# Where a pair's KT transposes stand among its scores, and a pause between two products of the joins

## The chip, the core and the metric

The kernel runs on one core of a Trainium2 chip. The metric is the device time of one execution in microseconds. A separate profiled execution gives the page of the profile and the trace. PE is TensorE, DVE is VectorE, ACT is ScalarE, POOL is GpSimd and SP is SyncE.

## The reference

One layer of a hybrid trunk over 16 + 512 = 528 tokens of width 1024. A combined projection feeds an RWKV-7 branch (eight heads of 64), a forgetting-attention branch (eight heads of 64) and the gates. Their gated sum and a residual follow, then an MLP with squared ReLU.

```python
u = rmsnorm(h, norm_mix[l])
proj = u @ w_in[l]
...
y_rw = rwkv7_branch(feat_rw, ...)
y_fx = fox_branch(feat_fx, b_f[l], q_gain[l], k_gain[l])
merged = gates[..., :D_MODEL] * (y_rw @ w_out_rw[l]) + gates[..., D_MODEL:] * (y_fx @ w_out_fx[l])
h = h + (merged @ w_o[l]).astype(h.dtype)
z = rmsnorm(h, norm_mlp[l])
h = h + (jnp.square(jax.nn.relu(z @ w_up[l])) @ w_down[l]).astype(h.dtype)
```

The part that the change touches is the recurrence of the RWKV-7 branch:

```python
def step(S, inp):
    rt, wt, kt, vt, at, bt = inp
    sa = jnp.einsum('bhij,bhj->bhi', S, at)
    S = S * wt[:, :, None, :] + sa[..., None] * bt[:, :, None, :] + vt[..., None] * kt[:, :, None, :]
    yt = jnp.einsum('bhij,bhj->bhi', S, rt)
    return S, yt
```

## The kernel before

The first stage computes everything from the input norm to the two branches and the gates; the later stages are the output projections and the MLP. The change lies in the first stage.

**The recurrence in chunks.** Tokens are padded to nine chunks of 64. The eight heads form four pairs, and two pairs form a group, so that there are two groups. For each pair, `keys` (L900) makes the scaled keys: BK on DVE (L922) and POOL, and on DVE (L924) KT, which is BK times the chunk's last decay. `rows` (L928) makes the left sides L0 and L1. `scores` (L952) then does, for three chunks at a time, 12 products of BK with L into two banks named psr (L964). DVE reads them out, masked, into Bm (L965) and back into L (L967, two operations). It also transposes KT of the same three chunks into a bank pbt (L971), from which ACT copies bkT in three operations (L972 and L974). bkT is read only by the chain.

`inverse` (L976) inverts, for a whole group, the triangular blocks which Bm holds. DVE first inverts blocks of 16 (L1001 and L1002), in tiles that take over the places of BK and KT; POOL clears the one at KT's place (L984 and L985). The joins then put the blocks together with products on PE of 32 rows: a first product p1 from Bm and Dn (L1027), read by DVE into W2 (L1028); a second, p1 from Tt and W2 (L1033); a third, p2 from W2 and Tt (L1036). DVE adds the second to Dn (L1037) and the third to Tt (L1041). Two more products follow (L1049 and L1056). `chain` (L1060) then goes through the nine chunks one after the other.

**Who sets the order on PE.** Within this stage the order of PE's instructions is the program's order, which a planner in the kernel writes while the program is built. Each piece of work is a generator. Between two yields it issues one *visit*, a few products and what reads them. The yielded function tells when, by the planner's clock, the next visit could start: when its inputs are ready and its PSUM banks are free. `Turns.run` (L167) takes the first stream, by rank, whose time plus a room for its rank isn't past the clock, and then books the issued instructions (`ck.read`, L186):

```python
ROOM = {0: 0.0, 1: 0.8, 2: 1.5, 3: 1.5, 4: 2.5, 8: 0.5}
...
at = next((i for i, t in enumerate(times) if t + self.ROOM[self.streams[i][0]] <= ck.pe + ck.SLACK), None)
```

SLACK is 0.15. The ranks are 0 for a chain, 1 for the recurrence's preparation (`recurrent`, L1187, with all of `keys`, `rows`, `scores` and `inverse`), 2 for attention, 3 for attention's features, 4 for the group norms and the splitting of results, and 8 for the input projections (L556). A visit of the projections is three or six products of the lines L582, and needs only its weights and a bank of its own.

The planner books DVE, ACT, POOL and the DMA with a fixed and a per-column time (L68); a product on PE by its columns and the size of its tile (L127), with 0.1 where the tile's shape changes. Operations that write a `wlo`, the rest of a weight after its upper half is taken off, are booked on POOL (L116); they are issued to DVE. The order on DVE, ACT and POOL is not the planner's but that of the framework's own scheduling.

**PSUM.** The tag "sm" has four banks, shared by psr, pbt, pw and most others. `banks(n)` (L507) gives the time at which the n oldest of the ring are free. The projections use "pj" (two banks) and borrow two more while no chain runs.

**The queues.** The projections' weights come over SP's DMA queue. Neither `scores` nor `inverse` issues a DMA.

Of the kernel before, what the change touches and what calls it, by code (L numbers as in the profile page):

```python
# [24 lines left out]
NCH = 9  # L25
# [30 lines left out]
def bc(ap, dim, n):  # L56

    shape = list(ap.shape)
    shape.insert(dim, n)
    return ap.unsqueeze(dim).to_broadcast(shape)  # L60
# [129 lines left out]
def kernel(ctx, tc, ht, x, win, par, cst, gain, lora, wout, wo, wup, wdn, out, dbg=None):  # L190
# [97 lines left out]
    with ExitStack() as st:  # L288
# [5 lines left out]
        def psm(name="psm"):  # L294
            return ps.tile([128, 512], F32, name=name, tag="sm", bufs=4)
# [22 lines left out]
        ck = Clock(nc)  # L318
# [188 lines left out]
        def banks(n):  # L507
            return ck.ring("sm", n, 4)
# [346 lines left out]
        class Pair:  # L855
# [96 lines left out]
            def scores(self):  # L952


                BK, L, KT = self.BK, self.L, self.KT
                self.bkT = bkT = kp.tile([128, NCH, 128], F32, name="bkT", bufs=2)
                self.Bm = Bm = kp.tile([128, NCH, 128], F32, name="Bm", bufs=2)
                for c0 in range(0, NCH, 3):
                    yield lambda: max(ck.ready(BK, *L) if c0 == 0 else 0.0, banks(2))
                    sb, sk = [psm("psr").rearrange("p (a b) -> p a b", b=128) for e in range(2)]  # L960
                    for j in range(3):
                        for sp, row, turn in ((sb, 0, 1), (sk, 1, -1)):
                            for (e, hs), os in zip(enumerate(hss), hss[::turn]):
                                mm(sp[os, j, :], BK[hs, c0 + j, row, :], L[e][hs, c0 + j, :], start=True, stop=True)  # L964
                    V.tensor_tensor(Bm[:, c0:c0 + 3, :], sb[:, :3, :], bc(tmask, 1, 3), ALU.mult)  # L965
                    for e, os in enumerate(hss[::-1]):
                        V.tensor_tensor(L[e][os, c0:c0 + 3, :], sk[os, :3, :], bc(tmask[os], 1, 3), ALU.mult)  # L967
                    yield lambda: max(ck.ready(KT) + 1.0, banks(1))
                    pb = psm("pbt").rearrange("p (a b) -> p a b", b=128)
                    for c in range(c0, c0 + 3):  # L970
                        nc.tensor.transpose(pb[:, c - c0, :], KT[:, c, :, :].rearrange("p a b -> p (a b)"), ident)  # L971
                    A.copy(bkT[:, c0:c0 + 3, :64], pb[:, :3, :64])  # L972
                    for hs, os in zip(hss, hss[::-1]):
                        A.copy(bkT[hs, c0:c0 + 3, 64:], pb[os, :3, 64:])  # L974

        def inverse(g, Bms, late):  # L976
# [40 lines left out]
            def half(q):  # L1017
                return qs[q % 2]
# [12 lines left out]
            for n, pr_, c in cells:  # L1031
                for e, hs in enumerate(hss):
                    mm(p1[hs, n, :], Tt[qs[2 * e], c, pr_, :], W2[qs[2 * e], n, :], start=True, stop=True)  # L1033
            for n, pr_, c in cells:
                for q in range(4):
                    mm(p2[qs[q], n, :], W2[qs[q], n, :], Tt[qs[q], c, pr_, half(q)], start=True, stop=True)  # L1036
# [150 lines left out]
        def recurrent():  # L1187
# [4 lines left out]
            for g in range(2):  # L1192
                prs = pairs[2 * g:2 * g + 2]
                for j, q in enumerate(prs):
# [19 lines left out]
                    if j == 0 and g > 0:  # L1214
                        yield normalised[0][1]
                    yield from q.bonus()
                yield from inverse(g, [q.Bm for q in prs], (lambda: pairs[2].ask_keys(inverted[0])) if g == 0 else lambda: None)
                inverted[g].done = True
                turns.add(0, chain(g, prs))
# [396 lines left out]
```

## Time and profile before

| what | value |
|---|---|
| median of three runs | 828.11 us (827.68 to 828.64) |
| profiled execution | 826.71 us |
| its span, first to last instruction | 824.9 us |
| mean granted clock of TensorE | 0.998 |
| first stage, 0 to 400 us: PE, DVE, ACT busy | 388.30, 298.40, 250.04 us |
| 400 to 495 us: PE, DVE, ACT busy | 93.92, 55.61, 48.35 us |
| 495 us to the end: PE, DVE, ACT busy | 325.94, 253.75, 154.10 us |

The visits of the scores (L964) lie at 52.6 to 60 us for pair 0, 84.8 to 94 for pair 1, 209.9 to 224 for pair 2 and 251.3 to 259 for pair 3. The joins' products (L1027 to L1056) lie at 114 to 130 us and at 283 to 299 us.

In a line of the time line the first number is the start in microseconds, the second the duration; a group of like instructions is merged, with its count behind an x. In brackets stand the idle time of the engine before it, and who ended it. The products are pipelined, so that what one costs is read from the start of one to the start of the next, not from its duration. A product of fp32 operands appears as more than one PE instruction.

### The profile page before, as it was taken

To read this page: it belongs to the slowest core of one execution; us is meant where nothing else is said; L and a number is where in the kernel's file an instruction comes from. 1 tells how busy PE (TensorE), PEld (TensorE's weight loads), DVE (VectorE), ACT (ScalarE), POOL (GpSimd) and SP (SyncE) were. 2 spreads that over 40 slices of the span, in tenths; PEclk is the share of its full clock that TensorE was granted. 3 is DMA by queue.
4 is the path that set the end of the run, shared out by engine and by line. 5 is a ranking of instruction groups with operands and counts; after the bars stand their busy time and mean duration, and the time that the engine had idled before them with its cause. 6 is when DMAs were issued, how large, how long until landed. Compare 5 with 4: busy or idle time off the path is not lost.

```text
span 824.9 us, 15506 instructions
## 1 busy us (share of the span) xinstructions
PE 808.1 (98%) x5886; PEld 667.3 (81%) x5886; DVE 607.8 (74%) x1196; ACT 452.5 (55%) x941; POOL 120.0 (15%) x124
## 2 busy tenths in 40 slices
PE   8999999998999999999999999999999999999998
PEld 6979887876987886778788889888888888888886
DVE  6797985687779855975267655875698678867988
ACT  7767548766575457664366534664445434543452
POOL 1021000010011000000022003100740174017400
PEclk9999999999999999999999999999999999999999
DMA  7222221211211311223687404533742365236532
GB/s 240 75 71 79 69 92 56 79 40 65 79 52 54 128 46 61 90 66 116 218 289 226 159 0 151 176 82 100 225 150 87 115 221 150 77 118 208 156 107 76
DMA packets 51483, 95.88 MB, mean 116 GB/s; under 512 B 5832, under 2 KB 7240, under 8 KB 51408
## 3 DMA queue, kind: packets, MB, share of 16 engines
q1 hardware_dynamic: 47680, 86.37, 33.0%
q0 software_dynamic: 1280, 4.20, 1.7%
q10 hardware_dynamic: 2448, 4.33, 1.5%
q8 instruction: 46, 0.75, 0.4%
q14 instruction: 29, 0.24, 0.1%
HBM read 88.56 MB, written 6.31 MB: 115 GB/s over the span
## 4 chain that ended last, share of the span: by engine, by line
PE 86%; DVE 5%; ACT 5%; issue 2%; DMA 1%; POOL 0%; DVEq 0%; ACTq 0%; SPq 0%
PE pj L582 22%; PE po L1357 21%; PE po L1484 12%; PE pd L1484 5%; PE po L1267 4%; PE po L1329 3%; PE pj L394 1%; PE pd L1298 1%; PE po L1298 1%; PE psc L751 1%; PE py L805 1%; PE psr L964 1%; PE ppt L788 1%; DVE wlo L551 1%; PE pch L1115 1%
## 5 line engine op out<-in xcount | busy, mean ns | idle before, releaser
L582 PE MATMUL pj<-uhi,whi 128*128 128x264 f32 (+1 forms) x480 | 164.3, 342 | 0.0
L582 PE MATMUL pj<-uhi,wlo 128*128 128x264 f32 (+1 forms) x480 | 153.9, 321 | 1.8 <-DVE wlo L551 1.8
L582 PE MATMUL pj<-ulo,whi 128*128 128x264 f32 (+1 forms) x480 | 153.8, 320 | 0.0
L242 DVE TENSOR_TENSOR wlo<-wraw,whi 128x512 fp32r<-128x512 f32 x84 | 81.0, 973 | 36.8 <-ACT whi L242 36.8
L582 PEld LDWEIGHTS pj<-uhi,whi 128*128 128x128 f32 x480 | 90.7, 189 | 12.9 <-issue 4.4
L582 PEld LDWEIGHTS pj<-uhi,wlo 128*128 128x128 f32 x480 | 90.7, 189 | 8.8 <-DVE wlo L551 2.2
L582 PEld LDWEIGHTS pj<-ulo,whi 128*128 128x128 f32 x480 | 91.0, 190 | 6.7 <-issue 1.6
L1357 PE MATMUL po<-zhi,whi 128*128 128x512 f32 (+1 forms) x248 | 94.8, 382 | 0.0
L1357 PE MATMUL po<-zlo,whi 128*128 128x512 f32 (+1 forms) x248 | 94.8, 382 | 0.0
L1357 PE MATMUL po<-zhi,wlo 128*128 128x512 f32 (+1 forms) x248 | 94.8, 382 | 0.0
L242 ACT CAST whi<-wraw 128x512 fp32r<-128x512 f32 x84 | 51.4, 617 | 53.5 <-PE po L1357 20.3
L551 DVE TENSOR_TENSOR wlo<-wraw,whi 128x512 fp32r<-128x512 f32 x78 | 53.8, 699 | 23.5 <-ACT whi L550 22.6
L550 ACT CAST whi<-wraw 128x512 fp32r<-128x512 f32 x78 | 47.7, 617 | 42.4 <-PE pj L582 41.7
L276 ACT CAST whi<-t 128x512 fp32r<-128x512 f32 x64 | 39.9, 624 | 44.6 <-DVE wlo L276 27.2
L1406 POOL TENSOR_TENSOR t<-traw 128x512 f32<-128x512 f32 x24 | 38.4, 1622 | 173.6 <-DMA traw<-in_wdn 173.6
L1484 PE MATMUL po<-wlo,fhi 128*128 128x512 f32 (+1 forms) x164 | 63.4, 387 | 0.2
L1484 PE MATMUL po<-whi,flo 128*128 128x512 f32 (+1 forms) x164 | 62.8, 384 | 0.0
L1484 PE MATMUL po<-whi,fhi 128*128 128x512 f32 (+1 forms) x164 | 62.3, 384 | 0.0
L276 DVE TENSOR_TENSOR wlo<-t,whi 128x512 fp32r<-128x512 f32 x64 | 43.5, 689 | 24.3 <-ACT whi L276 24.0
L1373 ACT CAST fhi<-R 128x768 fp32r<-128x768 f32 (+1 forms) x32 | 30.2, 945 | 49.1 <-DVE R L1380 26.1
L1357 PEld LDWEIGHTS po<-zlo,whi 128*128 128x128 f32 x248 | 46.6, 188 | 9.1
L1357 PEld LDWEIGHTS po<-zhi,wlo 128*128 128x128 f32 x248 | 46.6, 188 | 9.0
(330 smaller groups left out, 1706.4 us busy)
## 6 DMA issues: line engine op xcount, KB each, us to landing
wraw<-in_win SPq DMA_DIRECT2D x84, 256.0 KB, 2.6
wraw<-in_wup SPq DMA_DIRECT2D x60, 256.0 KB, 3.1
wraw<-in_wdn SPq DMA_DIRECT2D x48, 256.0 KB, 2.7
traw<-in_wdn SPq DMA_DIRECT2D x48, 256.0 KB, 3.5
gd<-gt ACTq DMA_DIRECT2D x16, 256.0 KB, 2.2
wraw<-in_wout SPq DMA_DIRECT2D x16, 256.0 KB, 3.9
gl<-gd SPq DMA_DIRECT2D x16, 256.0 KB, 3.8
traw<-in_wdn POOLq DMA_DIRECT2D x16, 256.0 KB, 3.1
```

The source lines that it names most:

```text
L242: casts.append((A.copy(hi, raw), low.tensor_tensor(lo, raw, hi.bitcast(F32), ALU.subtract)))
L276: return A.copy(hi, x), V.tensor_tensor(lo, x, hi.bitcast(F32), ALU.subtract)
L550: after(A.copy(hi, raw), last["ACT"])
L551: low[0] = V.tensor_tensor(lo, raw, hi.bitcast(F32), ALU.subtract)
L582: mm(po, a, b[:, k, a0:a1], start=n == 0, stop=n == 23)
L1267: mm(po, a, ys[k][:, b, :], start=n == 0, stop=n == 11)
L1298: mm(pd[i], a[:, k, 128 * i:128 * i + 128], b, start=k == 0 and n == 0, stop=k == 7 and n == 2)
L1329: mm(po, a[:, k, 128 * i:128 * i + 128], b[:, k, :], start=n == 0, stop=n == 23)
L1357: mm(po[:, t0:t1], a, b[:, k, t0:t1], start=n == 0, stop=n == 23)
L1373: A.copy(fhi[:, j, a:b], R[:, a:b])
L1406: eng.tensor_tensor(t, sums[c, pair] if c in (T1, T2) else c, d, ALU.add)
L1484: mm(x[i][:, cols], a[:, k, left, 128 * rows:128 * rows + 128], c[:, cols], start=start and k == 0 and n == 0, stop=stop and k == n_pairs ...
```

## The change

In `scores`, the loop over the three groups of chunks is cut in two. Before, each turn held a visit of scores and then a visit of transposes. Now there are three visits of scores and then three visits of transposes, and the transposes' yield no longer adds 1.0 us to KT's time.

In `inverse`, a yield comes in between the joins' second and third product. It takes the planner's clock as it stands before the second product is booked.

```diff
@@ -965,7 +965,8 @@
                     V.tensor_tensor(Bm[:, c0:c0 + 3, :], sb[:, :3, :], bc(tmask, 1, 3), ALU.mult)
                     for e, os in enumerate(hss[::-1]):
                         V.tensor_tensor(L[e][os, c0:c0 + 3, :], sk[os, :3, :], bc(tmask[os], 1, 3), ALU.mult)
-                    yield lambda: max(ck.ready(KT) + 1.0, banks(1))
+                for c0 in range(0, NCH, 3):
+                    yield lambda: max(ck.ready(KT), banks(1))
                     pb = psm("pbt").rearrange("p (a b) -> p a b", b=128)
                     for c in range(c0, c0 + 3):
                         nc.tensor.transpose(pb[:, c - c0, :], KT[:, c, :, :].rearrange("p a b -> p (a b)"), ident)
@@ -1031,6 +1032,8 @@
             for n, pr_, c in cells:
                 for e, hs in enumerate(hss):
                     mm(p1[hs, n, :], Tt[qs[2 * e], c, pr_, :], W2[qs[2 * e], n, :], start=True, stop=True)
+            at = ck.pe
+            yield lambda: at
             for n, pr_, c in cells:
                 for q in range(4):
                     mm(p2[qs[q], n, :], W2[qs[q], n, :], Tt[qs[q], c, pr_, half(q)], start=True, stop=True)
```

## The prediction

> **What bounds the kernel now.** I read the page first, then busy time by stretches, the waits of PE, and last the order of time around the edited places.
>
> ```profile
> span 824.9 us, 15506 instructions
> PE 808.1 (98%) x5886; PEld 667.3 (81%) x5886; DVE 607.8 (74%) x1196; ACT 452.5 (55%) x941; POOL 120.0 (15%) x124
> ```
>
> PE has work in 808.1 of 824.9 us. Its idle time is 16.8 us in all, so a change that only reorders PE's work has at most that to gain, and can lose by new idle time and by dearer changes between kinds of product. Busy time by stretches (stretch, length, then PE, PEld, DVE, ACT, POOL):
>
> ```profile
> 52.00:60.00 8.00, 8.00 (x100) 5.92 (x99) 6.88 (x14) 4.17 (x11) 0.14 (x1) 1.00 0.48 154
> 86.00:94.00 8.00, 7.04 (x82) 5.68 (x83) 7.85 (x15) 3.48 (x11) 1.09 (x2) 1.00 0.32 100
> 131.00:208.00 77.00, 73.27 (x680) 56.43 (x679) 58.45 (x182) 53.37 (x146) 3.95 (x8) 0.98 0.20 65
> 370.00:400.00 30.00, 30.00 (x142) 24.86 (x139) 14.99 (x34) 13.33 (x24) 0.00 (x0) 1.00 0.39 126
> ```
>
> The edited code runs in the first 400 us. The last 30 us of these (fourth row) hold no idle time: gate projections, which need nothing of the recurrence, end the stage. An earlier or later recurrence therefore doesn't itself move the end; a microsecond counts where PE stands still or does something slower. Pair 0's scores (first row) have no idle time, pair 1's (second) 0.96 us. Who made PE wait (total, times, longest):
>
> ```profile
> PE pbt L971 <- DVE KT L924: 2.1, 2, 1.3
> ...
> PE pch L1115 <- DVE Rs L1111: 1.7, 3, 1.2
> ...
> PE psr L964 <- DVE Bm L965: 0.4, 1, 0.4
> ```
>
> The first row is the wait that the change addresses: the transposes come up on PE before DVE has scaled KT. The last belongs to the same scores.
>
> **The waits of the scores.** Pair 1, PE, then DVE:
>
> ```profile
> 84.84 0.89 PE L964 MATMUL psr<-L,BK 64*64 64x128 f32 x24 [0.28 <-DVE BK L922]
> 86.51 0.55 PE L971 MATMUL pbt<-cs,KT 128*128 128x128 f32 x3 [0.78 <-DVE KT L924]
> ...
> 88.59 0.87 PE L964 MATMUL psr<-L,BK 64*64 64x128 f32 x20 [0.45 <-DVE Bm L965]
> ```
>
> ```profile
> 85.10 1.35 DVE L924 TENSOR_TENSOR KT<-BK,P 128x1152 f32<-128x1152 f32 x1
> ...
> 86.77 1.28 DVE L551 TENSOR_TENSOR wlo<-wraw,whi 128x512 fp32r<-128x512 f32 x2
> 87.98 0.55 DVE L965 TENSOR_TENSOR Bm<-psr,cs 128x384 f32<-128x384 f32 x1
> ...
> 88.56 1.12 DVE L967 TENSOR_TENSOR L<-psr,cs 64x384 f32<-64x384 f32 x2
> ```
>
> PE waited 0.78 us for KT and later 0.45 us for a bank that DVE had not yet read out. The planner books the weights' rests (wlo) on POOL, while the trace has them on DVE: here 1.28 us of them stand ahead of Bm, so DVE is later than planned. Pair 3, PE with the projections between, then DVE:
>
> ```profile
> 251.26 0.89 PE L964 MATMUL psr<-L,BK 64*64 64x128 f32 x24
> 253.46 0.52 PE L971 MATMUL pbt<-cs,KT 128*128 128x128 f32 x3 [1.31 <-DVE KT L924]
> 253.73 0.37 PE L582 MATMUL pj<-uhi,whi 128*128 128x264 f32 x1
> 253.93 0.28 PE L582 MATMUL pj<-ulo,whi 128*128 128x264 f32 x1
> ...
> 254.29 0.28 PE L582 MATMUL pj<-ulo,whi 128*128 128x264 f32 x1
> 254.41 0.28 PE L582 MATMUL pj<-uhi,wlo 128*128 128x264 f32 x1
> 254.62 0.89 PE L964 MATMUL psr<-L,BK 64*64 64x128 f32 x24
> 255.44 0.39 PE L582 MATMUL pj<-uhi,whi 128*128 128x264 f32 x1
> 255.67 0.28 PE L582 MATMUL pj<-ulo,whi 128*128 128x264 f32 x1
> ```
>
> ```profile
> 253.91 0.55 DVE L965 TENSOR_TENSOR Bm<-psr,cs 128x384 f32<-128x384 f32 x1
> 254.49 1.12 DVE L967 TENSOR_TENSOR L<-psr,cs 64x384 f32<-64x384 f32 x2
> ```
>
> These rows give the prices, from start to start. A projection product takes 0.12 us (254.29 to 254.41), a visit of six 0.72. A visit of scores takes 0.82 (254.62 to 255.44). Entering the 64*64 shape costs 0.09 (254.41 to 254.62 is 0.21, less 0.12), leaving it 0.11 (255.44 to 255.67), and the first projection after transposes 0.08 (253.73 to 253.93).
>
> What goes: the KT waits, 0.78 + 1.31 = 2.09 us, because three visits of scores now lie ahead of the first transpose, and the split visit's 0.45, because the second visit no longer comes where it stood.
>
> What is late next: a visit of scores takes two of the four banks "sm", so the first two visits may stand side by side and the third needs the banks of the first, which DVE frees with one Bm and two L operations. By the planner's rates for these three (L68) and its room of 0.80 - 0.15 us, some 2 us of other work fit in before the third visit: I put in three projection visits. In pair 1 the third then comes at 84.84 + 2 x 0.82 + 0.11 + 3 x 0.72 + 0.09 = 88.84, and its banks are free at 88.56 + 1.12 = 89.68: a new wait of 0.84. In pair 3 it comes at 251.26 + 4.00 = 255.26 against 254.49 + 1.12 = 255.61: 0.35. In pair 0 KT was early, and in pair 2 both visits come behind a long stretch of projections, so I put nothing there. The bounds: nothing at all if DVE takes Bm ahead of the rests, and 1.28 us more (the two rests) if a second pair of rests falls in between. I take 0.84 + 0.35 = +1.19.
>
> [...]
>
> **Changes of shape.** With two visits of scores side by side one leaving and one entering go, 0.20 a pair; transposes that stand alone cost 0.08 each more. I take -0.10 a pair, -0.40 for four; the bounds are 0 and -0.80.
>
> The transposes issue nine products and nine ACT copies a pair, as before, and no DMA; ACT, busy 3.48 of the 8 us in the second row of the stretches, has room for them in a row; the queues of SP and POOL are not passed by any of them. One thing waits for the last of them, POOL's clearing of the inverse's start, which reuses KT's place:
>
> ```profile
> 259.90 0.29 POOL L985 MEMSET AX<- 128x32 f32 x1
> ```
>
> ```profile
> 263.61 0.19 DVE L1001 TENSOR_TENSOR tmp<-AX,AX 128x30 f32<-128x30 f32 x1
> ```
>
> It is done 3.4 us before DVE needs it, so a microsecond's delay is hidden; past 3.4 us DVE's inverse would be late, still with projections for cover.
>
> **The joins.** First inverse, PE:
>
> ```profile
> 117.64 2.05 PE L1033 MATMUL pw<-AX,Tt 32*64 32x32 f32 x64
> 119.62 1.29 PE L1036 MATMUL pw<-Tt,AX 32*32 32x32 f32 x128
> 120.84 0.50 PE L582 MATMUL pj<-uhi,whi 128*128 128x512 f32 x1
> 121.17 0.39 PE L582 MATMUL pj<-ulo,whi 128*128 128x512 f32 x1
> 121.40 0.40 PE L582 MATMUL pj<-uhi,wlo 128*128 128x512 f32 x1
> ...
> 123.95 1.20 PE L1049 MATMUL pw<-AX,Bm 32*32 32x32 f32 x64
> ```
>
> The new yield returns the planner's time from before the second product (L186 reads the clock after the yield). The planner books 0.53 us for these 32 products (32 columns at a quarter of 1/600 us each, and 0.1 for the shape), less than the 0.65 us of room, so one other visit, most likely a projection's, comes in between. The visit itself would run anyway. Its price is two more changes of shape, each 0.10 (120.84 to 121.17 is 0.33, against 0.23 to 121.40): +0.20, twice +0.40. The third product is late by about 0.9 us, and so is the next step; the trace's 3.1 us between the third product's end (120.84) and L1049 move with it, under cover of projections. The bounds: 0 if no visit comes in, +0.80 if two do.
>
> [...]
>
> **The sum.** -2.09 - 0.45 + 1.19 - 0.40 + 0.40 = -1.35 us. The profiled execution took 826.71 us (1.8 beside its span), which gives 825.36; the median of the runs shown, 828.11, stands 1.40 above it, which gives 826.76.
>
> **The rivals.**
>
> The waits go and nothing takes their place: DVE takes Bm ahead of the rests, or more projections come in before the third visit. Then the 1.19 falls away: -2.54, 825.6 us. For it: pair 0's 8 us without a wait. Against it: the order on DVE in pair 1.
>
> Slower, by the first chain. Everything after the first join is planned anew, and the chain runs in 131 to 208 us, where PE stood idle for 77.00 - 73.27 = 3.73 us, the Rs row above being its largest part; there Rs is copied on DVE, in one queue with the unbooked rests. If the new order makes that idle time twice what it was, the sum is -1.35 + 3.73 = +2.4: 830.5 us. It decides from 2.9 - 3.0 us of added idle time on (1.35 + 1.66, the latter 0.2%). Against it: before the change this order had its waits already, so as much may go as come.
>
> The change doesn't do what it says: the banks hold the second visit of scores back until KT is scaled and DVE's reading out sets PE's pace as KT did; the waits stay, the joins' 0.40 comes on top: 828.5 us. For it: in pair 1 all three waits are for the same late engine.
>
> **How the numbers follow.** A measurement of this kernel can tell about 0.2%, 1.66 us, from no change. The forecast, 826.8 us, gets 0.45 (its own range 825.9 to 828.2, mostly within 0.2%, 0.10 of it below); nothing in place of the waits 0.27 (nearly all faster); the chain 0.13 (slower); no effect 0.15 (within, 0.03 slower). Together: faster 0.35, the same 0.50, slower 0.15. The range reaches down to the first rival with the shapes at their bound and the 0.28 us wait for BK gone (825.6 - 0.40 - 0.28 = 824.9), and up to the third with another 1.1 us wait for banks: 825.0 to 829.6.
>
> **What would show it.** No row of PE waiting for KT; a wait of psr for Bm or L of about 0.8 us in pair 1 and 0.3 in pair 3, right before the third visit; the first two visits side by side; a projection's visit between L1033's and the third product; the idle time of 131 to 208 us near 3.7. If that last number moves by more than 2 us, it outweighs the rest and the forecast is wrong, whichever way the scores went.

## The result and the profile after

The changed kernel takes **846.98 us** (845.19 to 848.84) against 827.89 for the kernel before in the same series: a ratio of 1.0232, with a 95% interval of 1.0201 to 1.0263, so 19.1 us slower. The prediction was 826.8 us, with a range of 825.0 to 829.6. Its profiled execution took 848.84 us at a mean granted clock of 0.985 (before: 826.71 us at 0.998); it is the slowest of the four, whose clocks run from 0.992 down to 0.985.

The head of the page of the changed kernel:

```profile
span 847.1 us, 15512 instructions
...
PE 818.7 (97%) x5886; PEld 673.8 (80%) x5886; DVE 611.2 (72%) x1196; ACT 458.9 (54%) x945; POOL 120.3 (14%) x124
```

The span grew by 22.2 us, in two halves of about the same size. Idle time of PE is 847.1 - 818.7 = 28.4 us against 16.8: +11.6. The same 5886 products took 818.7 us instead of 808.1: +10.6. PE got no more work; the clock was lower. By the mean clocks, 0.015 x 847.1 = 12.7 us of full-speed time were lost, against 0.002 x 824.9 = 1.6 before.

Who made PE wait, changed kernel (total, times, longest):

```profile
PE pyt L1171 <- DVE ysq L1166: 8.3, 1, 8.3
...
PE pbt L972 <- DVE Bm L965: 2.0, 2, 1.4
...
PE psr L964 <- DVE Bm L965: 1.3, 1, 1.3
...
PE psr L964 <- DVE L L967: 1.2, 2, 0.8
```

There is no row for KT: that wait is gone, as meant. In its place stand waits of scores and transposes for Bm and L, 2.0 + 1.3 + 1.2 us in these rows (0.5 more in a smaller one), and one wait of 8.3 us in another place altogether, the first group norm's transposes (pyt) for their input ysq.

Busy time by stretches (the columns are those of the prediction, with the granted clock third from the end):

```profile
52.00:60.00 8.00, 7.37 (x96) 5.36 (x94) 7.80 (x17) 3.66 (x10) 0.14 (x1) 1.00 0.44 142
86.00:94.00 8.00, 5.90 (x87) 4.83 (x87) 7.85 (x17) 1.50 (x5) 0.14 (x1) 0.81 0.34 99
131.00:208.00 77.00, 66.92 (x696) 52.44 (x694) 49.42 (x145) 47.94 (x128) 3.82 (x7) 0.93 0.19 59
391.00:421.00 30.00, 30.00 (x143) 23.22 (x142) 14.94 (x34) 12.84 (x23) 0.00 (x0) 1.00 0.36 115
```

Pair 0's scores now have 0.63 us of idle time and pair 1's 2.10 (before: none and 0.96), the latter with the clock at 0.81. Between 131 and 208 us PE stands idle for 77.00 - 66.92 = 10.08 us instead of 3.73. The stage ends as before in 30 us without a gap, but at 421 instead of 400 us.

**Pair 1's scores.** PE of the changed kernel, then DVE:

```profile
86.43 1.54 PE L964 MATMUL psr<-L,BK 64*64 64x128 f32 x48
87.90 0.39 PE L582 MATMUL pj<-uhi,whi 128*128 128x264 f32 x1
...
88.61 0.28 PE L582 MATMUL pj<-uhi,wlo 128*128 128x264 f32 x1
90.18 0.44 PE L964 MATMUL psr<-L,BK 64*64 64x128 f32 x4 [1.28 <-DVE Bm L965]
91.43 1.55 PE L964 MATMUL psr<-L,BK 64*64 64x128 f32 x20 [0.81 <-DVE L L967]
```

```profile
86.90 1.35 DVE L924 TENSOR_TENSOR KT<-BK,P 128x1152 f32<-128x1152 f32 x1
...
88.97 0.68 DVE L551 TENSOR_TENSOR wlo<-wraw,whi 128x512 fp32r<-128x512 f32 x1
89.57 0.55 DVE L965 TENSOR_TENSOR Bm<-psr,cs 128x384 f32<-128x384 f32 x1
```

The first two visits do stand side by side (x48). Between the second and the third there is **one** projection visit, six products from 87.90 to 88.61, not three. DVE takes KT first, then other work and a weight's rest, and starts the first Bm at 89.57. So PE waits 1.28 us before the third visit and, inside it, another 0.8 for L. These 2.09 us in pair 1 are as much as the two KT waits that went (0.78 + 1.31).

**The first group norm.** PE, then DVE:

```profile
180.38 0.28 PE L582 MATMUL pj<-uhi,wlo 128*128 128x264 f32 x1
188.99 1.08 PE L1171 MATMUL pyt<-cs,ysq 128*128 128x128 f32 x4 [8.33 <-DVE ysq L1166]
```

```profile
182.56 1.35 DVE L924 TENSOR_TENSOR KT<-BK,P 128x1152 f32<-128x1152 f32 x1
...
184.38 0.69 DVE L551 TENSOR_TENSOR wlo<-wraw,whi 128x512 fp32r<-128x512 f32 x1
...
186.16 0.68 DVE L551 TENSOR_TENSOR wlo<-wraw,whi 128x512 fp32r<-128x512 f32 x1
...
188.16 0.69 DVE L1166 TENSOR_TENSOR ysq<-y_rw,rsgy 128x512 f32<-128x512 f32 x1
```

In the kernel before, ysq was written at almost the same time, but its transposes stood on PE 10 us behind that (DVE, then PE):

```profile
186.82 0.69 DVE L1163 TENSOR_TENSOR ysq<-y_rw,rsgy 128x512 f32<-128x512 f32 x1
```

```profile
197.77 0.65 PE L1168 MATMUL pyt<-cs,ysq 128*128 128x128 f32 x4
```

So DVE did not become slower there; the planner put the norm's transposes 17 us earlier on PE, into a time in which DVE, with the next pair's keys and two rests in its queue, could not be done.

**What an idle PE costs behind its wait.** Busy time and granted clock around that wait and at the other low places of the changed kernel, then around the one low place of the kernel before:

```profile
91.40:94.80 3.40, 3.37 (x31) 3.07 (x32) 3.26 (x7) 0.94 (x3) 0.00 (x0) 0.57 0.11 39
180.00:183.40 3.40, 0.66 (x6) 0.46 (x4) 3.37 (x8) 1.42 (x4) 0.14 (x1) 0.95 0.00 0
183.50:193.80 10.30, 4.81 (x30) 4.24 (x31) 7.51 (x22) 2.49 (x8) 1.88 (x2) 0.52 0.16 52
224.50:227.90 3.40, 3.40 (x19) 3.40 (x18) 1.23 (x3) 1.80 (x7) 0.00 (x0) 0.56 0.01 4
248.40:251.80 3.40, 3.40 (x19) 3.40 (x19) 3.15 (x14) 0.83 (x2) 0.00 (x0) 0.56 0.53 178
303.00:306.40 3.40, 3.40 (x133) 2.60 (x133) 1.02 (x4) 0.00 (x0) 0.00 (x0) 0.56 0.37 127
```

```profile
200.10:203.50 3.40, 1.88 (x16) 1.02 (x12) 3.13 (x13) 1.04 (x3) 0.00 (x0) 0.95 0.00 0
203.50:206.90 3.40, 3.40 (x25) 3.21 (x22) 3.21 (x11) 2.34 (x5) 0.28 (x2) 0.55 0.09 31
```

In the norm's wait, which lasts from 180.66 to 188.99 us, the clock fell to half and stayed there beyond it, at 0.50 from 183.09 to 193.33 us (0.52 to 0.57 in the rows are 0.50 with a little of the neighbours); in the kernel before it was at 0.50 once, for 3.41 us from 203.17 us on, behind 3.40 - 1.88 = 1.52 us of idle time. In the changed kernel four pieces of 3.41 us come on top, from 90.93, 224.05, 247.95 and 302.56 us on: those at 91 and 224 us stand behind the waits of pair 1's and pair 2's scores, and the one at 303 us behind no wait at all (see the end). Of these 10.2 + 4 x 3.4 = 23.8 us at half clock PE was busy in 4.34 + 2.92 + 3.29 + 2 x 3.41 = 17.4, at a cost of 8.7 us, 7.0 more than the one piece of the kernel before (3.41 us, all busy): two thirds of the 10.6 us by which the products took longer; the rest was not told apart.

### The profile page after: what moved, and what is told of

It reads as the page before. It is cut to its first block, busy times and chain, and to the rows that moved or that the text cites. A ratio compares the mean times of both kernels' runs of the same rounds, so it can differ in the third digit from the quotient of the medians.

```text
span 847.1 us, 15512 instructions
## 1 busy us (share of the span) xinstructions
PE 818.7 (97%) x5886; PEld 673.8 (80%) x5886; DVE 611.2 (72%) x1196; ACT 458.9 (54%) x945; POOL 120.3 (14%) x124
## 4 chain that ended last, share of the span: by engine, by line
PE 68%; DVE 3%; ACT 2%; issue 1%; DVEq 0%
PE po L1360 21%; PE pj L582 13%; PE po L1487 12%; PE po L1270 5%; PE pd L1487 5%; PE po L1332 3%; PE pd L1301 1%; PE po L1301 1%; PE py L805 1%; PE psc L751 1%; PE ppt L788 1%; PE pd L1322 0%; DVE L L967 0%; PE pch L1118 0%; PE py L802 0%
## 5 line engine op out<-in xcount | busy, mean ns | idle before, releaser
L582 PE MATMUL pj<-uhi,whi 128*128 128x264 f32 (+1 forms) x480 | 166.4, 347 | 0.0
L242 DVE TENSOR_TENSOR wlo<-wraw,whi 128x512 fp32r<-128x512 f32 x84 | 84.8, 1020 | 33.7 <-ACT whi L242 32.5
L551 DVE TENSOR_TENSOR wlo<-wraw,whi 128x512 fp32r<-128x512 f32 x78 | 54.9, 712 | 29.2 <-ACT whi L550 28.7
L1360 PEld LDWEIGHTS po<-zhi,whi 128*128 128x128 f32 x248 | 46.6, 188 | 9.0
```

Of the source, the lines that this page charges most:

```text
L242: casts.append((A.copy(hi, raw), low.tensor_tensor(lo, raw, hi.bitcast(F32), ALU.subtract)))
L551: low[0] = V.tensor_tensor(lo, raw, hi.bitcast(F32), ALU.subtract)
L582: mm(po, a, b[:, k, a0:a1], start=n == 0, stop=n == 23)
L1360: mm(po[:, t0:t1], a, b[:, k, t0:t1], start=n == 0, stop=n == 23)
```

## The experiments

Ratios are to the kernel before, with their 95% intervals; it took 826.2 to 827.1 us (medians) beside these runs.

### Which of the two edits

e1: the changed kernel without the pause.

```diff
-            at = ck.pe
-            yield lambda: at
```

> The scores' edit alone, without the pause in the joins. Theory S (the scores' edit brings the loss: PE comes too early to the third visit, and the re-planned first group norm stalls PE for 8 us): 844 to 849 us, about 19 above the kernel before, with the 8.3 us wait for ysq in it. Theory J (the pause in the joins re-plans what follows and brings the loss): 825 to 829 us, no wait for ysq over 1 us.

e2: the kernel before with the pause alone.

```diff
+            at = ck.pe
+            yield lambda: at
```

> The pause in the joins alone, scores as before. Theory S: within 0.4% of the kernel before, 826 to 831 us, KT waits of 2.1 us as before. Theory J: 840 us and more, with a wait for ysq of several us.

e1 took 846.23 us (1.0235, 1.0215 to 1.0254), with the wait for ysq again 8.3 us. e2 took 829.23 us (1.0031, 1.0021 to 1.0041). The scores' edit holds the whole loss. The pause alone cost 2.7 us, not the 0.40 of the prediction; two things carry it in the trace. One is the chain's y_rw, for which PE waits 1.17 us at 344.7 us. The other is the clock behind a wait that was there before, too (the weight's rest, 1.80 us, at 51 us); kernel before, then e2:

```profile
46.16:49.57 3.41, 2.78 (x22) 2.35 (x20) 3.41 (x6) 2.59 (x6) 1.96 (x3) 1.00 0.09 24
49.57:52.98 3.41, 2.24 (x17) 1.66 (x21) 3.41 (x7) 0.96 (x2) 0.85 (x3) 1.00 0.38 114
52.98:56.39 3.41, 3.41 (x58) 2.52 (x50) 3.29 (x8) 1.75 (x5) 0.00 (x0) 1.00 0.59 193
```

```profile
48.71:52.13 3.42, 1.62 (x9) 1.06 (x8) 3.42 (x4) 1.24 (x3) 2.16 (x2) 1.00 0.01 2
52.13:55.54 3.41, 3.41 (x30) 2.23 (x29) 2.49 (x7) 1.15 (x2) 0.14 (x1) 0.50 0.76 231
```

The pause lies behind this place; the same wait was followed by half the clock in one execution (0.50 from 52.13 to 55.54 us in e2) and by full clock (1.00) in the other. What tells the two apart was not shown.

### The wait for ysq

e3: the norm's operations up to ysq issued at high priority, for the first norm only; the order on PE is that of the changed kernel.

```diff
+            with tc.high_priority() if g + c0 == 0 else nullcontext():
-            st1 = rp.tile([128, 2, 4], F32, name="st1")
+                st1 = rp.tile([128, 2, 4], F32, name="st1")
...
-            V.tensor_tensor(yn.rearrange("p i a d -> p a i d"), y, bc(rs, 3, 64), ALU.mult)
+                V.tensor_tensor(yn.rearrange("p i a d -> p a i d"), y, bc(rs, 3, 64), ALU.mult)
```

> The changed kernel with the first group norm's operations on DVE and ACT at high priority; the planner's order on PE stays the same. If the 8.3 us wait and the half clock right after it are a part of the loss by themselves: the wait for ysq falls under 3 us, the half-clock stretch from 183 to 194 us shrinks, and the time falls by 6 to 11 us to 836 to 841. Rival, DVE is late as a whole in this stretch: what is taken ahead delays others, the wait moves to other rows and the time falls by less than 3 us, 844 and more.

843.19 us (1.0198, 1.0168 to 1.0228). PE in e3:

```profile
187.46 1.09 PE L1172 MATMUL pyt<-cs,ysq 128*128 128x128 f32 x4 [6.59 <-DVE ysq L1167]
```

The wait fell by 1.7 us only, and the time lies between the two expectations; its interval overlaps that of the changed kernel. The author's guess at the reason, not tested, is that DVE's queue was full of work that others needed as soon (in the changed kernel DVE was busy in 3.37 of the 3.40 us from 180.00 us on), and that the norm is a chain of small operations that wait for one another.

e5 and e9: the same kernel twice, 36 products that nobody reads ahead of the norm's transposes, so that PE is busy while DVE finishes. Of the first only the times are used.

```diff
-            pt = psm("pyt").rearrange("p (a b) -> p a b", b=128)
+            pt = psm("pyt")
+            if g + c0 == 0:
+                for i in range(36):
+                    mm(pt, uhi[:, 0, :128], uhi[:, 0, :512], start=True, stop=True)
+                ck.seen = len(nc.cur_bb.bb.instructions)
+            pt = pt.rearrange("p (a b) -> p a b", b=128)
```

> The changed kernel with 36 products of 0.23 us, whose result nobody reads, on PE in front of the first group norm's transposes, unbooked by the planner, so that the order of everything else stays: they fill the 8.3 us in which PE waited for ysq. Theory C (idle time itself makes the clock fall to half, and this costs beyond the wait): the half-clock stretch of 10.2 us from 183 to 194 us goes, and the time falls by 2 to 3 us to about 844.5. Rival (the clock falls for another reason, such as the share of small tiles): the stretch stays and the time stays at 847 or rises.

> The changed kernel with 36 products of 128 columns and fp32 operands, read by nobody and not booked by the planner, put on PE right ahead of the first group norm's product: they add work that is not part of the computation. It is the kernel of the experiment before on the same question, whose profile fell in a disturbed execution; here the question is the profile. The wait for ysq in the changed kernel was 8.3 us, with the granted clock at 0.50 from 183.5 to 193.8 us. Theory (the wait itself lowers the clock): with PE kept busy the wait for ysq falls under 2 us, no stretch at 0.50 lies between 180 and 195 us, and the mean granted clock of the span is above 0.990. Rival (the clock falls for another reason, such as the mixture of small products around it): the stretch at 0.50 stays where it was, and the mean stays near 0.985. Time 841 to 846 us by either, since the filling takes the place of the wait and only the halved clock behind it can be saved.

e5 gave 1.0194 (1.0168 to 1.0219), e9 841.31 us, 1.0179 (1.0158 to 1.0199). PE and a window of e9:

```profile
180.10 8.36 PE L1171 MATMUL pyt<-uhi 128*128 128x512 f32 x36
188.63 0.63 PE L1176 MATMUL pyt<-cs,ysq 128*128 128x128 f32 x4 [0.17 <-DVE ysq L1166]
```

```profile
184.00:188.00 4.00, 4.00 (x19) 3.34 (x18) 3.77 (x13) 0.00 (x0) 1.92 (x2) 1.00 0.27 84
```

The products are 512 columns wide, as the row shows, not 128 as the expectation has it. Useless work in the place of the wait makes the kernel faster by 1.0232 - 1.0179 = 0.0053, or 4.4 us (by e5's times 3.1 us): the stretch behind the wait is back at full clock (1.00 from 180 to 200 us), and the mean clock is 0.998. So the wait cost more than its own 8.3 us; in the changed kernel PE was busy in 4.34 of the 10.24 us at half clock, which makes 2.2 us more. How much exactly, these runs don't say. In the profiled execution of e9 the halved pieces at 224, 248 and 303 us are gone too (1.00 from 220 to 260 and from 280 to 320 us), though nothing was changed there, and the 3.1 and 4.4 us rest on a few executions whose clocks differ.

e7: the planner books the weights' rests on DVE, where they run.

```diff
-            eng = "Pool" if out.startswith("wlo") else str(x.engine).split(".")[-1]
+            eng = str(x.engine).split(".")[-1]
```

> The changed kernel with the planner booking the weights' rests on DVE, where they run, instead of on POOL. If DVE's unbooked load is why the planner lets PE come too early to the group norm and to the third visits: the wait for ysq falls under 2 us and the waits of psr and pbt for Bm and L under 2 us together, 830 to 838 us. Rival, the planner now holds PE back where DVE has room, so that products are moved to where nothing covers them: 840 and more.

852.54 us (1.0304, 1.0285 to 1.0322), a miss. Waits of PE in e7:

```profile
PE pw L1028 <- DVE AX L1014: 12.7, 2, 7.5
...
PE pyt L1171 <- DVE ysq L1166: 1.5, 1, 1.5
```

The wait for ysq does fall, from 8.3 to 1.5. That doesn't show that the unbooked rests caused it, since e11 and e13 below lose that wait with the rests booked as before. And the new plan puts the joins' first product too early, for 12.7 us. One booking made true does not make a plan better while others are false.

### The planner's clock

The source says why one projection visit came in and not three. The planner knows a tile by its name, not by the columns that are read or written, and a product's start is its latest input's:

```python
deps = max([self.w.get(n, 0.0) for n in names] + [self.free.get(out, 0.0)])
...
    self.pe = end = max(self.pe, deps) + cost
```

The second visit reads chunks of L that nobody has changed, but L was just written for the first three chunks (L967). The visit's yield asks only for banks, so the planner lets it go at once; booking it then pushes the planner's clock to the end of that writing. The planner believes that this time has passed, sees the banks of the third visit free, and puts in few projections. By the rates of L68 one Bm and two L operations are booked with 3 x 0.59 us, and 0.15 to hand over: the second visit is booked 1.9 us later than PE can do it. Its own products take 0.64 us by L127, just under the room of 0.65, so one projection visit comes in and then the third visit is due. On the chip the second visit doesn't wait, and the third comes up too early (in pair 1 PE waits 1.28 us ahead of it, as above). In the kernel before, transposes and projections stood between two visits, and the jump was smaller. This is the source's own arithmetic; whether the loss hangs on it is what the next runs ask.

e4: each visit waits, in its yield, for L.

```diff
-                    yield lambda: max(ck.ready(BK, *L) if c0 == 0 else 0.0, banks(2))
+                    yield lambda: max(ck.ready(BK, *L), banks(2))
```

> The changed kernel, but the second and third visits of scores also wait, by the planner's clock, until L has been written by the visit before (the planner books L as one tile, and its clock jumps by up to 2 us when a visit is issued ahead of that). If this jump is why too few projections stand before the third visit: projections come in between the visits, the waits of psr for Bm and L and of pbt for Bm fall from 5 us in all to under 2, and the half-clock stretches at 91 and 224 us go: at least 5 us faster than the changed kernel, 842 or less, more if the group norm is planned otherwise. Rival, DVE is late whatever the planner's clock says: the same waits stay, 845 to 849.

e6: e4 without the pause.

> The scores' edit alone, with each visit of scores waiting until L has been written by the visit before; no pause in the joins. If the planner's jump was the scores' whole fault and the pause costs its 2 us here too: 827 to 831 us, no wait of pbt for KT, and none of psr or pbt for Bm or L above 0.5 us. Rival, the transposes behind all scores cost something of their own: 833 and more.

e4 took 831.51 us (1.0056, 1.0039 to 1.0073): no wait for KT, Bm, L or ysq, so some 15 us of the loss are gone. What is left is a new wait, for the norm of the next pair's keys, with half clock behind it (0.53 over 6.80 us; waits and window of e4):

```profile
PE pkk L909 <- ACT sq L905: 3.5, 1, 3.5
```

```profile
76.30:83.10 6.80, 5.68 (x23) 5.28 (x24) 4.22 (x10) 5.87 (x11) 1.40 (x1) 0.53 0.17 43
```

e6 took 833.3 us (1.0076, 1.006 to 1.0093). That is a miss: its time lies where its rival was expected, though no wait for KT, Bm or L is left. It waits 4.3 us for the next keys' norm, 3.7 for Rs and 1.8 for BK, so what these yields cost lies elsewhere in the plan. Against e4 the pause looks rather like a gain, but the two intervals overlap.

e13: the jump itself is taken out. L's time is set back, at each visit, to that of the rows' writes; nothing else of the change is touched.

```diff
+                w0 = {}
                 for c0 in range(0, NCH, 3):
                     yield lambda: max(ck.ready(BK, *L) if c0 == 0 else 0.0, banks(2))
+                    w0 = w0 or {l.tensor.name: ck.w[l.tensor.name] for l in L}
+                    ck.w.update(w0)
```

> The changed kernel, with the planner's time for L set back, at each visit of scores, to what the rows' writes gave it, so that the second and third visit are no longer booked as waiting for the visit before. The order written by the planner then has the first two visits of scores side by side and three projection visits ahead of the third one (pair 0), as the prediction assumed. Theory (the loss is the jump: places too early for real time, after it the wait for ysq): waits of PE for Bm and L in the scores under 1.5 us in total, no wait for KT, no wait for ysq above 2 us, time 824 to 834 us. Rival (three visits of scores ahead of the transposes are dear by themselves, whatever the planner believes, since DVE reads their banks out no faster): waits for Bm and L stay at 3 us or more, and the time is 838 us or more.

**825.94 us** (824.92 to 829.41; 0.9986, 0.9974 to 0.9998). PE in pair 1:

```profile
87.77 1.54 PE L967 MATMUL psr<-L,BK 64*64 64x128 f32 x48
89.25 0.39 PE L582 MATMUL pj<-uhi,whi 128*128 128x264 f32 x1
...
91.39 0.28 PE L582 MATMUL pj<-uhi,wlo 128*128 128x264 f32 x1
91.60 0.43 PE L967 MATMUL psr<-L,BK 64*64 64x128 f32 x4
92.77 0.87 PE L967 MATMUL psr<-L,BK 64*64 64x128 f32 x20 [0.74 <-DVE L L970]
```

Two visits side by side, 18 products of projections from 89.25 on (three visits), and a wait of 0.74 us in the third visit: in pair 1 this is the order that the prediction drew up, with its 0.84. Elsewhere the plan differs: in pair 3 one projection visit stands between the first two visits and two ahead of the third, and in pair 2 the second and third stand side by side; neither waits for its scores. No wait for KT, none for ysq. At this SLACK the loss goes with the jump, and the edit itself stays as it was.

### What a new plan does by itself

The long wait for ysq lies 90 us behind pair 1's scores. Is it the jump's, or would any edit have drawn something like it? e10 and e12 are the kernel before with another SLACK in the planner, e11 the changed kernel with another SLACK. e15 is the kernel before with the jump taken out as in e13; e14 and e18 are e13 and e15 with SLACK 0.20.

```diff
-    SLACK = 0.15
+    SLACK = 0.20
```

(in e12 0.10)

> The kernel before with the planner's SLACK at 0.20 instead of 0.15: the computation and the edited code are as before, but nearly every place in the order on PE can move. Theory (the loss belongs to the scores' edit, by the jump of the planner's clock): a plan made anew without that edit costs little, 823 to 833 us. Rival (any plan made anew loses about as much, since the one before was a lucky one): 838 to 850 us.

> The changed kernel with the planner's SLACK at 0.20 instead of 0.15. The jump of the planner's clock at the second and third visit of scores stays, the places of the rest move. Theory: the waits of the scores for Bm and L stay (2 us or more together in the first two pairs), and the planner's belief that time has passed still places something too early; where it hits differs, so the 8.3 us wait for ysq may go, and the time is 834 to 848 us, at least 6 us above the kernel before with the same SLACK. Rival (the 8.3 us wait was an accident of one plan and is the whole loss): without it 824 to 831 us, within 3 us of the kernel before with the same SLACK.

> The kernel before with SLACK at 0.10 instead of 0.15, the second plan made anew without the edited code. Theory (plans made anew cost a few us either way, and the scores' edit is what costs about 19): 823 to 833 us. Rival (the spread of plans is itself some 20 us): 838 to 850 us, or more than 10 us away from the one with SLACK 0.20.

> The same, with SLACK at 0.20. The changed kernel took 830.75 us with this SLACK, with 6.3 us of waits of PE for Bm and L in the scores and the transposes; the kernel before took 825.18. Theory: without the jump those waits fall under 2 us, and the time comes to 823 to 828 us. Rival (scores in a row are dear by themselves): the waits stay, 829 to 833 us.

> The kernel before with the same setting back of L's time: the control. There a transpose stood between two visits of scores, and the planner's clock jumped less. Theory: small, 823 to 832 us, with KT waits as before or more (nothing drives the transposes later). Rival (taking the jump out is itself worth several us in any kernel, by some other place in the plan): 822 us or less.

> The control for 823.77 us (the change without the jump, SLACK 0.20): the kernel before without the jump, SLACK 0.20. Theory (without the jump the edit itself is worth between -1.5 and +1.5 us): 822 to 826 us. Rival (the edit is worth more than its KT waits): 826 us or more.

Times in us; ratios to the kernel before, as it was, in the same series:

| | SLACK 0.15 | SLACK 0.20 |
|---|---|---|
| kernel before | 827.89 | e10 825.18, 0.9980 (0.9971 to 0.9990) |
| changed | 846.98, 1.0232 (1.0201 to 1.0263) | e11 830.75, 1.0048 (1.0032 to 1.0064) |
| before, no jump | e15 824.83, 0.9971 (0.9961 to 0.9981) | e18 825.95, 0.9992 (0.9982 to 1.0002) |
| changed, no jump | e13 825.94, 0.9986 (0.9974 to 0.9998) | e14 823.77, 0.9959 (0.9944 to 0.9975) |

Waits of PE in e11:

```profile
PE psr L964 <- DVE Bm L965: 2.9, 2, 1.5
...
PE psr L964 <- DVE L L967: 2.2, 3, 0.8
...
PE pbt L972 <- DVE L L967: 1.2, 3, 0.7
```

Read down the right column: with the jump the edit costs 830.75 - 825.18 = 5.6 us, without it it gains 0.9992 - 0.9959 = 0.0033, or 2.7 us (against e10 1.7). That is more than the 1.5 us that e18's theory allowed, though its time lies in that theory's bounds. In e11 there is no wait for ysq, and 6.3 us of waits for Bm and L in these rows. It missed the bounds of both theories by a little (6 us or more, 3 or less); the waits are as the first had them. Its two halved pieces, one at 57 us behind these waits and one between 80 and 100 us (clock 0.92 from 40 to 60 us, 0.91 from 80 to 100), are in the 5.6 us. So the edit with the jump costs 5.6 us without the ysq wait, and that wait with the clock behind it 8.3 + 2.2 = 10.5; the two make 16.1 of the 19.1, but they come from two plans. The rows of the changed kernel itself give: scores and transposes 5.0 us of waits and 3.1 of clock behind them (91 and 224 us), ysq 10.5, the pieces at 248 and 303 us 3.4, less 2.5 of waits and 1.7 of clock that the kernel before had: 17.8 of the 22.2 us by which the profiled span grew.

e12, at SLACK 0.10, took 834.95 us (1.0108, 1.0089 to 1.0127) though nothing of it was edited: its plan has two waits of 2.2 and 2.3 us for pm and one of 2.0 for nm, both of the attention, and a mean clock of 0.991. It missed the 823 to 833 that were expected, and lies 9.8 us from e10, close to the 10 that its rival named. A new plan can thus cost 9 us (0.0108 of 826.4) by itself, which is why one number with one plan says little of an edit.

### The pause and the KT waits by themselves

e17 is e13 without the pause.

> The changed kernel without the planner's jump (825.94 us with the pause), and without the pause between the joins' second and third product: the edit of the scores alone, as the prediction priced it. Theory (the 2.7 us that the pause cost alone were a stretch of the granted clock at 0.50, tripped by chance of the phase, and the pause itself is worth under 1 us): 824.5 to 827 us. Rival (the pause costs its 2 to 3 us here as well): 822 to 824 us.

825.56 us (0.9988, 0.9976 to 0.9999): the pause makes no difference that can be told here.

e8 is the kernel before with the transposes asked for later; e16 is the same at SLACK 0.20.

```diff
-                    yield lambda: max(ck.ready(KT) + 1.0, banks(1))
+                    yield lambda: max(ck.ready(KT) + 3.0, banks(1))
```

> The kernel before, its order of scores and transposes kept, with 3.0 in place of 1.0 us added to KT's time. If the KT waits are worth their idle time and the rest of the plan holds: no wait of pbt for KT, about 2 us faster than the kernel before (ratio 0.997). Rival, the new plan brings other waits: same or slower, up to 1% or more, whatever becomes of the KT waits.

> The kernel before with the transposes' time 3.0 instead of 1.0 us behind KT and SLACK at 0.20. With SLACK 0.15 the 3.0 us gave 0.9972 of the kernel before; with 1.0 us and SLACK 0.20 the time was 825.18 us, with 2.4 us of KT waits. Theory (the KT waits themselves are worth their 2 us, in any plan): no wait for KT and 822 to 824.3 us. Rival (the gain was one lucky plan): 825 us or more.

e8 took 824.41 us (0.9972, 0.9958 to 0.9985), e16 824.7 us (0.9968, 0.9954 to 0.9983); neither has a wait for KT. At SLACK 0.15 that is 2.3 us less by the ratio (1.2 to 3.5), about the waits' 2.09; at 0.20 it is 1.0 us less than e10 by the ratios, between the two expectations. So the KT waits can be taken out by one number in one line, without the change. e8, e10 and e13 to e17 are faster than both kernels, none by more than half a per cent of the kernel before; e14, with 0.9959, is the fastest.

## Why the prediction was wrong

**The KT waits** (-2.09) went, as said: no row of PE waits for KT. The second visit's 0.45 us went, too; it now stands beside the first.

**The third visit's wait** (+0.84 in pair 1, +0.35 in pair 3, none in 0 and 2) rested on one sentence: "By the planner's rates for these three (L68) and its room of 0.80 - 0.15 us, some 2 us of other work fit in before the third visit: I put in three projection visits." **This is the step that failed.** The rates of DVE's operations were right (0.59 us booked for each, 0.55 and 0.56 in the trace), but the second visit's booking moves the planner's clock itself; one visit came in. Two visits less are 2 x 0.72 = 1.44 us on top of the 0.84; pair 1 waited 2.09 us. Pair 2, priced at nothing, waited 2.0 (the pbt row for Bm above): its second and third visit stand side by side, and the transposes come right behind them. Pairs 0 and 3 waited 0.6 and 0.3 us. Where three visits came in (e13, pair 1), 0.74 us were measured.

**The stretch of 131 to 208 us.** A second step failed here, and by size it is the larger: the sum put what the new plan does to everything behind the scores, and the clock, at nothing, and the runs showed 8.3 us of waiting for ysq and some 2 us for the halved clock behind it. The prediction had this only as the rival "slower, by the first chain". The rival had the right place, but the wrong wait (Rs, where it was ysq) and the wrong size: 3.73 us of idle time more, where 6.35 were measured. Its 830.5 us also lay outside the prediction's own range. The text's own test, "If that last number moves by more than 2 us, it outweighs the rest and the forecast is wrong", is what came about. It gave that rival 0.13.

**The price of a wait.** Each wait was counted as its own length. In the rows shown before, the mean clock of the 131 to 208 us was 0.98 and not 1.00, the mark of its halved piece; the prediction drew nothing from it. In the changed kernel the halved pieces made up 7.0 of the 22.2 us by which the span grew.

**Changes of shape** (-0.40): not told apart by any run; too small beside what the plans do.

**The pause** (+0.40, bounds 0 to 0.80): "one other visit, most likely a projection's, comes in between" was right. Joins of the first group in the changed kernel:

```profile
120.05 2.05 PE L1034 MATMUL pw<-AX,Tt 32*64 32x32 f32 x64
122.04 1.12 PE L683 MATMUL pssq<-fsq,cs 128*128 128x512 f32 x2
123.09 1.29 PE L1039 MATMUL pw<-Tt,AX 32*32 32x32 f32 x128
```

It was one of the attention's features here. What the pause is worth depends on the plan: by the ratios +2.6 us (e2), -0.2 (e13 against e17), -0.2 (the changed kernel against e1) and -1.7 (e4 against e6); of these only e2's is clear of the intervals. Its own 0.40 can't be read out of that.

**The sum** of -1.35 us came out at -1.1 in e13 (825.94 against 827.06 beside it), where its assumption on the order holds. That is no proof of every term: e15 shows that taking the jump out is worth 2.4 us without the edit, and the edit without the jump is worth +1.1 us (e13 less e15, intervals overlapping) at one SLACK and -2.7 at the other.

**What stays open:** whether the jump causes the ysq wait in any sense beyond this plan. At SLACK 0.15 the changed kernel, e1 and e3 have it, and no kernel with the jump taken out or waited for (e4, e6, e13, e17) has; at SLACK 0.20 the jump is there without it (e11). Each of these is a plan made anew, and e12 shows that such a plan can gain or lose waits by itself.

## What to carry to other kernels

Where a planner writes the order, an edit is priced by what the planner will believe after it, not by the old trace with the pieces moved: follow its clock through the booking of each moved instruction, and look for a tile that is booked whole but used in parts. Judge such an edit in two or three plans (another slack, with a control that has the same slack and no edit), since a new plan alone moved this kernel by -2 to +9 us. And where the engine that bounds the kernel comes to stand still, look at the granted clock of the stretch behind it before calling the wait's length its price: here half clock came with the wait of 8.3 us, behind 1.52 us of idle time in the kernel before, and in some runs behind a wait of 1.80 us.

## What the runs showed of the hardware

Filling a wait of 8.3 us with useless products made the kernel 4.4 us faster (e9 against the changed kernel); the mean granted clock of the profiled execution was 0.998 instead of 0.985.

One and the same wait of 1.80 us, for the same operand, ending at 51 to 53 us, was followed by half clock in e2, e4, e13 and e17 (0.58, 0.60, 0.55 and 0.64 over the stretch from 52.70 to 56.10 us) and in e7 (the products of 512 columns behind it start 0.43 us apart, where e6 has 0.23), and by full clock, 1.00, in the kernel before and the changed one, e1, e6, e8, e9, e12 and e15. What tells them apart was not shown; the "phase" in the expectation of e17 was the author's guess, and no run set it. The length of the idle time alone does not tell: 1.52 us of it stood ahead of half clock in the kernel before (203 us), the 1.80 us ahead of full clock in these eight. Executions of one kernel differ in their clock, too: e13's ten run from 824.92 us at a mean clock of 1.000 to 829.41 at 0.996.

And PE need not look idle. In the changed kernel the piece at 303 us, at 0.50 from 302.56 to 305.97 us, follows a stretch without any wait, in which products of 32*64 of the second group's inverse stand (windows, then PE):

```profile
299.15:302.56 3.41, 3.41 (x70) 2.82 (x71) 2.00 (x10) 2.35 (x8) 0.00 (x0) 1.00 0.19 64
```

```profile
300.33 2.05 PE L1034 MATMUL pw<-AX,Tt 32*64 32x32 f32 x64
```

The same products at 117.64 us in the kernel before (clock 1.00 from 115.00 to 125.20 us), and those of the same inverse in e9 (1.00 from 280 to 320 us), had no halved piece behind them, so why the clock fell there stays open.
